# A hybrid S5 and retention layer on one core: a single-column product ahead of each S5 chunk's transposes, and four smaller moves

## The chip, the cores and the metric

The kernel runs on one core of a Trainium2 chip. The metric is the device time of one execution in microseconds (us); three executions of the kernel before gave 1423.64 to 1424.38, with a median of 1424.18. One more execution was profiled and took 1424.95, of which the profile's span is 1423.2.

## The reference, cut to what matters

One layer of a hybrid network works on 256 prompt tokens and on 8 samples of 8 tokens each, 320 in all, with D = 2048:

```python
h = rms_norm(x, norm_mix)
u, q, k, v, g = split(h @ w_in)            # 1024 columns each
bu = einsum(u in 64 groups of 16, b_bar)   # S5: a 64-dim complex state per group
xs = associative_scan(lam_bar, bu); y = Re(einsum(xs, c)) + d * u
y = gelu(y); s5_out = y * sigmoid(y @ w_glu + b_glu)
# retention: 8 heads, rotary positions, decay, group norm
scores = (rotary(q) @ rotary(k)) * mask
o = scores @ v + (q @ r) * q_decay;  r_new = r * decay + (k * k_decay) @ v
ret_out = silu(g) * group_norm(o)
x = x + concat(s5_out, ret_out) @ w_out
x = x + (silu(gate) * up) @ w_ffn_out      # gate, up = split(rms_norm(x) @ w_ffn_in)
```

All of it is float32; the S5 and retention states after the last token are outputs too.

## The kernel before, in words

Every large product is `weights x activations` with the 320 tokens as columns. A weight load brings 8 tiles of 128x128 (512 KB) into `raw`. ScalarE rounds it into `hi` (the CAST at L133), VectorE subtracts to get `lo` (L135), and TensorE runs three products per tile: hi with the rounded activations (L145), hi with their rest (L146), lo with the rounded ones (L147). `raw`, `hi` and `lo` have three buffers each, so a load waits until the subtraction three loads earlier has freed its `raw`, and that one waits until TensorE has freed its `lo`.

The input projection `w_in` is 40 blocks of 128 columns: 8 for u, then q, k, v, g for each of the 8 heads. Each block is 16 tiles, 48 products into `ps_p`. Between these products TensorE runs the small work: retention for 8 heads (`head_k`: transposes `pst`, scores `pss`; `head_v`: transposes `pst2`, outputs `po` and `psr`, transposes `pn`) and S5 for 8 chunks of 8 groups (`s5_chunk`). After it come w_out, the GLU, the FFN and the final norm, which the change doesn't touch.

An S5 chunk c goes like this. ScalarE copies its part of u to `up_`; SP writes that to DRAM (`via`, L586) and reads it back in eight transfers (L590) into `kst`, each into 16 of its 128 rows, which lays the four time steps of a window below one another. `kst` has two buffers. VectorE builds `bl` and `cl` from the chunk's parameters. After a delay `b1`, TensorE transposes `bl` into `pt` (four at L109), and ScalarE copies them to `bst`. After a further delay `b2` come the outputs of the chunk before (`s5_outputs`, products of `kst`, `toe` and `cl`, `xp` into `py`) and the chunk's own products of `bst` with `kst` into `pb`. The last columns of `pb` give the first block of `toe`; six transfers (L654) shift it into place. VectorE then scans (`s5_scan`). For the last chunk the outputs follow in the same function after a delay `scan`.

What sets the order: TensorE and POOL run in the order in which the program emits them. A planner emits it: `clk.now` adds an estimated cost for each product (0.4 per tile of a projection, 0.04 to 0.43 for the small ones), and generators such as `s5_chunk` and `head_k` come back at a due time (`yield DL[...]`: b1 14.2, b2 6.6, scan 17.8), when `run_due` finds them between two tiles. VectorE, ScalarE and SP are ordered by the framework with priorities (`tc.high_priority(offset=...)`, weight loads highest) and by `tc.issue_after`. SP issues all loads and transfers of the projection from one queue, in one order, and each instruction in it that must wait holds those behind it.

`make_identity` and `ones` are the constants for the transposes and for eight products (`warm_ps`, L118) that TensorE runs first of all. `rot` turns q and k of a head (three VectorE operations); `vsp` collects the sample part of v of two heads (L770).

Of the kernel before, what the change touches and what calls it, by code (L numbers as in the profile page):

```python
# [46 lines left out]
def hybrid_kernel(ctx, tc, xT, w_in, w_in4, w_out, w_glu, w_fi, w_fo, w_fot, gfr, vecs, s5p, bc, x0,  # L47
# [11 lines left out]


    ident = cst.tile([P, P], F32, name="ident")
    make_identity(nc, ident)
    ones = cst.tile([P, P], F32, name="ones")
    pool.memset(ones, 1.0)
    mhalf = cst.tile([P, 4], F32, name="mhalf")
    pool.memset(mhalf, -0.5)
    vec = cst.tile([P, vecs.shape[1]], F32, name="vec")
# [35 lines left out]
    def mm(cost, *a, **k):  # L103
        pe.matmul(*a, **k)
        clk.now += cost
# [471 lines left out]
    def s5_chunk(c):  # L577
# [42 lines left out]
            tbl = s5_table(c)  # L620
        bst = s5.tile([P, 4, P], F32, name="bst", tag="bst", bufs=1)
        pt = misc("pt")
        for i in range(4):
            tr(pt[:, P * i:P * i + P], bl[:, i // 2, i % 2].rearrange("p u e h -> p (u e h)"))
        with tc.high_priority(offset=EVAC):
# [3 lines left out]
        if c:  # L629
            while clk.now - used["misc"] < MISC:  # L630
                yield 0.4
            pending.pop()()
        pb = ps_b.tile([P, 2, 512], F32, name="pb", tag="pb", bufs=1)
        for i in range(4):
            for u in range(2):

# [20 lines left out]
        if c < 7:  # L657
            pending.append(lambda: s5_outputs(c, kst, cl, xp))
            return
        yield DL["scan"]  # L660
        while clk.now - used["misc"] < MISC:
            yield 0.4
        s5_outputs(c, kst, cl, xp)
# [61 lines left out]
    def rot_(ps, name):  # L725
        sw = mp.tile([P, N], F32, name="sw", tag="sw", bufs=1)
        act.copy(sw[0:64], ps[64:128])
        rot_t["keys"] = act.copy(sw[64:128], ps[0:64])
        a = mp.tile([P, N], F32, name=name, tag=name, bufs=1)
        tt(a, ps, csr[:, 0], MUL)  # L730
        tt(sw, sw, csr[:, 1], MUL)
        tt(a, a, sw, ADD)
        return a

    def head_k(h, q_, qg, k_, R):
# [25 lines left out]
    def head_v(h, v_, qg, rt, R):  # L761
        yield DL["v"] + (3.0 if h == 0 else 0.0)
        pst2 = misc("pst2")
        for i, s in enumerate(STARTS):
            tr(pst2[:, P * i:P * i + P], v_[:, s:s + P])
        vT = mp.tile([P, 3, P], F32, name="vT", tag="vT", bufs=1)
        with tc.high_priority(offset=EVAC):
            for i in range(3):
                act.mul(vT[:, i], pst2[:, P * i:P * i + P], rtok[:, i:i + 1])
        act.copy(vsp[64 * (h % 2):64 * (h % 2) + 64], vT[64:128, 2])  # L770
        last = act.copy(vs[:, h], vT[64:128, 2])
        if h == 0:
            rot_t["values"] = last
            with tc.issue_after(last.ins):
                s5_powers()
            start_chunk(0)
        yield DL["o"]
        kd, sm = R["kd"], R["sm"]

        po = ps_v.tile([P, 4, P], F32, name="po", tag="po", bufs=1)  # L780
        mm(0.22, po[:, 0], sm[:, 0:P], vT[:, 0], start=True, stop=True)
        mm(0.22, po[:, 1], sm[:, P:256], vT[:, 0], start=True, stop=False)
        mm(0.22, po[:, 1], sm[:, 256:384], vT[:, 1], start=False, stop=True)
        nt = 2 + h % 2
        if h % 2:
            two = (HS[h - 1], R)
            mm(0.22, po[:, 2], smp, vsp, start=True, stop=False, skip_group_check=True)
            for j in range(4):
                for g in range(2):
                    for u in range(2):  # L790
                        r = 64 * g + 32 * u
                        mm(0.06, po[r:r + 32, 2], two[g]["qg"][:, u, 32 * j:32 * j + 32],
                           two[g]["rt"][:, 4 * u + j], start=False, stop=j == 3, tile_position=(0, r),
                           skip_group_check=True)
        st = mp.tile([P, 3, 6], F32, name="st", tag="st", bufs=1)
        mv = mp.tile([P, 2, 3], F32, name="mv", tag="mv", bufs=1)[:, :, 0:nt]
        y = mp.tile([P, 2, 3], F32, name="gy", tag="gy", bufs=1)[:, :, 0:nt]
        with tc.high_priority(offset=GN):
            for i in range(nt):
                dve.bn_stats(st[:, i], po[:, i])  # L800
                dve.bn_aggr(mv[:, :, i], st[:, i])

        m_, t_, y_, w_ = mv[:, 0], mv[:, 1], y[:, 0], y[:, 1]
        pool.tensor_scalar(m_, m_, -1.0, None, MUL)
        pool.tensor_scalar(t_, t_, EPS, None, ADD)
        pool.tensor_tensor(y_, t_, mhalf[:, 0:nt], ALU.pow)
        pool.tensor_tensor(w_, y_, y_, MUL)
        pool.tensor_tensor(w_, w_, t_, MUL)
        pool.tensor_scalar(w_, w_, -0.5, 1.5, MUL, ADD)
        pool.tensor_tensor(y_, y_, w_, MUL)  # L810
        pool.tensor_tensor(w_, m_, y_, MUL)
        if h == 0:
            rot_t["first"]()
        on = mp.tile([P, 3, P], F32, name="on", tag="on", bufs=1)

        def normed():
            with tc.high_priority(offset=EVAC):
                for i in range(nt):
                    act.activation(on[:, i], po[:, i], AF.Identity, scale=y[:, 0, i:i + 1],
                                   bias=y[:, 1, i:i + 1])  # L820

        if h:
            normed()
        psr = misc("psr")
        mm(0.22, psr[:, :P], kd[:, 0], vT[:, 0], start=True, stop=False)
        mm(0.22, psr[:, :P], kd[:, 1], vT[:, 1], start=False, stop=True)
        rp = mp.tile([P, P], F32, name="rp", tag="rp", bufs=1)
        with tc.high_priority(offset=EVAC):
            act.copy(rp, psr[:, :P])
        sp.dma_start(rp_o[h], rp)  # L830
        t0 = clk.now
        if not h:

            for _ in range(2):
                cast = last_hi[0]
                while last_hi[0] is cast:
                    yield 0.4
            with tc.issue_after(last_hi[0].ins):
                normed()
        yield max(2.0, DL["c"] - (clk.now - t0))  # L840
        pn = misc("pn")
        for i in range(nt):
            tr(pn[:, P * i:P * i + P], on[:, i])

        R["fused"] = R.get("sgt") is not None
        parts = [(h, pn[:, 0:NP], slice(0, NP))]
        if h % 2:
            parts += [(h - 1 + g, pn[:, NP + 64 * g:NP + 64 * g + 64], slice(NP, N)) for g in range(2)]
        with tc.high_priority(offset=EVAC):
            for i, a_, sl in parts:  # L850
                if HS[i]["fused"]:
                    stt(retp[:, i, sl], a_, v("gn", i), HS[i]["sgt"][:, sl], MUL, MUL)
                else:
                    act.mul(retp[:, i, sl], a_, v("gn", i))
        if h % 2:
            for R_ in two:
                R_["gn"] = True
                if R_["fused"]:
                    R_["sg"] = True
# [16 lines left out]
    def do_q(h, ps=None):  # L876
        ps = proj(8 + 4 * h) if ps is None else ps
        R = HS[h]
        rt = mp.tile([P, NB, P], F32, name="rt", tag="rt", bufs=2)
        R["rt"] = rt  # L880
        for i in range(2 if h == 1 else min(h, 1)):
            i = i if h == 1 else h
            with tc.issue_after(last_raw[0].ins) if h == 1 else nullcontext():
                sp.dma_start(HS[i]["rt"], r0[i])
        mk = mp.tile([P, NP + P], F32, name="mk", tag="mk", bufs=2)
        n = NP + P if h % 2 else NP
        with nullcontext() if h else tc.issue_after(last_raw[0].ins):
            sp.dma_start(mk[:, 0:n], masks[h, :, 0:n])
        R["mk"] = mk
        q_ = rot(ps, "q_")  # L890
        pool.tensor_copy(qsp[:, 64 * (h % 2):64 * (h % 2) + 64], q_[:, NP:N])
        qg = qgs[h % 2]
        for u in range(2):
            tt(qg[:, u].rearrange("p (b w) -> p b w", w=40)[:, :, 0:NS],
               q_[:, NP + 32 * u:NP + 32 * u + 32].rearrange("p (b t) -> p b t", t=NS),
               gqt[:, h].unsqueeze(1).to_broadcast([P, 4, NS]), MUL)
        R.update(q_=q_, qg=qg)
        run_due()

    def do_k(h, ps=None):  # L900
        ps = proj(9 + 4 * h) if ps is None else ps
        R = HS[h]
        k_ = rot(ps, "k_")
        pool.tensor_tensor(kvf[:, h], k_[:, NP:N].rearrange("p (b t) -> p b t", t=NS),
                           kdt[:, h].unsqueeze(1).to_broadcast([P, NB, NS]), MUL)
        pool.tensor_copy(ksp[:, 64 * (h % 2):64 * (h % 2) + 64], k_[:, NP:N])
# [82 lines left out]
    def finish_norm():  # L989
# [4 lines left out]
        with tc.high_priority(offset=EVAC):  # L994
            act.copy(rbc, rps)
            tt(csr[:, 0], csr[:, 0], rbc, MUL)
            turned = dve.tensor_tensor(csr[:, 1], csr[:, 1], rbc, MUL)
            tt(u32[:, 0], ps0, rbc, MUL)
            tt(u32[:, 1], ps1, rbc, MUL)
        rot_t["ready"] = True  # L1000

        with tc.issue_after(turned.ins):
            s5_params2(exps[1])

    spawn(finish_norm(), DL["nm"])

# [538 lines left out]
```

## Time and profile before

| | |
|---|---|
| median of three runs | 1424.18 us (1423.64 to 1424.38) |
| the profiled execution | 1424.95 us |
| its span | 1423.2 us |
| TensorE busy | 1415.5 us, 99% of the span, 10376 records |
| VectorE busy | 957.9 us, 67% |
| ScalarE busy | 606.5 us, 43% |
| POOL busy | 122.8 us, 9% |
| DMA, 16 engines | 267.07 MB, mean 188 GB/s |

A row of a timeline gives the start, the duration, the engine, the line, the operation, output and inputs, shapes, the number of instructions in the row, and in brackets the idle time before it with what ended it. A row of the waits view names the engine and line that waited, what it waited for, the total, the number of times and the longest. A row of the windows view has the stretch and its length, busy time (and instructions) of TensorE, its weight loads, VectorE, ScalarE and POOL, then the granted TensorE clock, the DMA share and the rate. `SPq` rows are the issues of transfers on SP's queue, not the transfers themselves; `PEld` rows are TensorE's weight loads.

### The profile page before, as it was taken

Reading aid. Unit: us, or ns where it says so; the run is one execution under the profiler, and the core shown is the slowest. Engines: PE = TensorE matmul, PEld = TensorE weight load, DVE = VectorE, ACT = ScalarE, POOL = GpSimd, SP = SyncE. Lnnn points to the kernel's source line nnn. Section 1 sums busy time; section 2 is a strip of 40 time slices with the busy share of each in tenths; the row PEclk is TensorE's granted clock in tenths of the full one; section 3 lists DMA queues with packets and bytes.
Section 4 is the critical chain, followed back from the end, with each engine's and each line's share of the span. In section 5 each row is a group of like instructions: output and inputs, shape, how many; then the busy total and the mean of one; then the engine's idle time right before and its main releaser. Section 6 shows DMA issues by size and latency. Waiting matters only on the chain.

```text
span 1423.2 us, 26196 instructions
## 1 busy us (share of the span) xinstructions
PE 1415.5 (99%) x10376; PEld 1406.6 (99%) x10376; DVE 957.9 (67%) x1842; ACT 606.5 (43%) x973; POOL 122.8 (9%) x194
## 2 busy tenths in 40 slices
PE   9999999999999999999999999999999999999998
PEld 8999999999999999999999999999999999999998
DVE  7979878787557747777777545767644677655453
ACT  6654555555455443333333333333333333334553
POOL 7720111110000000100001000000000000000002
PEclk9999999999999999999999999999999999999999
DMA  8554555555644466675666446666545765445542
GB/s 278 170 187 158 163 174 157 171 163 157 218 156 151 164 209 228 221 253 201 245 206 231 136 148 238 233 216 235 170 146 175 255 233 190 159 157 184 154 143 75
DMA packets 102316, 267.07 MB, mean 188 GB/s; under 512 B 27377, under 2 KB 42033, under 8 KB 102193
## 3 DMA queue, kind: packets, MB, share of 16 engines
q1 hardware_dynamic: 101904, 265.01, 55.9%
q8 instruction: 81, 1.33, 0.4%
q10 hardware_dynamic: 288, 0.39, 0.1%
q14 instruction: 43, 0.34, 0.1%
HBM read 254.44 MB, written 10.52 MB: 186 GB/s over the span
## 4 chain that ended last, share of the span: by engine, by line
PE 96%; DVE 2%; DMA 1%; ACT 1%; issue 1%; POOL 0%; SPq 0%; POOLq 0%; DVEq 0%; ACTq 0%
PE ps_fg L147 7%; PE ps_fu L147 7%; PE ps_fu L146 7%; PE ps_fg L146 7%; PE ps_fg L145 7%; PE ps_fu L145 7%; PE ps_fo L147 7%; PE ps_fo L145 7%; PE ps_fo L146 7%; PE ps_p L145 6%; PE ps_p L147 6%; PE ps_p L146 6%; PE ps_o L145 2%; PE ps_o L146 2%; PE ps_o L147 2%; PE ps_t L1342 1%
## 5 line engine op out<-in xcount | busy, mean ns | idle before, releaser
L133 ACT CAST hi<-raw 128x1024 fp32r<-128x1024 f32 (+1 forms) x410 | 397.8, 971 | 684.2 <-PE ps_fg L146 182.3
L135 DVE TENSOR_TENSOR lo<-raw,hi 128x1024 fp32r<-128x1024 f32 (+1 forms) x410 | 462.8, 1129 | 304.2 <-ACT hi L133 301.3
L147 PE MATMUL ps_fg<-hhi,lo 128*128 128x320 f32 x704 | 218.0, 310 | 0.0
L147 PE MATMUL ps_fu<-hhi,lo 128*128 128x320 f32 x704 | 217.9, 310 | 0.0
L145 PE MATMUL ps_fg<-hhi,hi 128*128 128x320 f32 x704 | 217.9, 310 | 0.0
L146 PE MATMUL ps_fu<-hlo,hi 128*128 128x320 f32 x704 | 217.9, 310 | 0.0
L145 PE MATMUL ps_fu<-hhi,hi 128*128 128x320 f32 x704 | 217.9, 310 | 0.0
L146 PE MATMUL ps_fg<-hlo,hi 128*128 128x320 f32 x704 | 217.9, 310 | 0.0
L145 PE MATMUL ps_fo<-ahl,hi 128*128 128x320 f32 x671 | 208.0, 310 | 0.0
L147 PE MATMUL ps_fo<-ahl,lo 128*128 128x320 f32 x671 | 207.7, 310 | 0.0
L146 PE MATMUL ps_fo<-ahl,hi 128*128 128x320 f32 x671 | 207.7, 310 | 0.0
L145 PE MATMUL ps_p<-xhi,hi 128*128 128x320 f32 x560 | 177.3, 317 | 0.0
L147 PE MATMUL ps_p<-xhi,lo 128*128 128x320 f32 x560 | 173.3, 309 | 0.0
L146 PE MATMUL ps_p<-xlo,hi 128*128 128x320 f32 x560 | 173.1, 309 | 0.0
L147 PEld LDWEIGHTS ps_fg<-hhi,lo 128*128 128x128 f32 x704 | 132.2, 188 | 0.0
L146 PEld LDWEIGHTS ps_fu<-hlo,hi 128*128 128x128 f32 x704 | 132.2, 188 | 0.0
L146 PEld LDWEIGHTS ps_fg<-hlo,hi 128*128 128x128 f32 x704 | 132.2, 188 | 0.0
L145 PEld LDWEIGHTS ps_fg<-hhi,hi 128*128 128x128 f32 x704 | 132.2, 188 | 0.0
L147 PEld LDWEIGHTS ps_fu<-hhi,lo 128*128 128x128 f32 x704 | 132.1, 188 | 0.0
L145 PEld LDWEIGHTS ps_fu<-hhi,hi 128*128 128x128 f32 x704 | 132.1, 188 | 0.0
L146 PEld LDWEIGHTS ps_fo<-ahl,hi 128*128 128x128 f32 x671 | 126.0, 188 | 0.0
L147 PEld LDWEIGHTS ps_fo<-ahl,lo 128*128 128x128 f32 x671 | 126.0, 188 | 0.0
(476 smaller groups left out, 2117.8 us busy)
## 6 DMA issues: line engine op xcount, KB each, us to landing
raw<-w_fi SPq DMA_DIRECT2D x176, 512.0 KB, 4.2
raw<-w_in SPq DMA_DIRECT2D x79, 512.0 KB, 4.1
raw<-w_fo SPq DMA_DIRECT2D x61, 512.0 KB, 3.5
raw<-w_out SPq DMA_DIRECT2D x32, 512.0 KB, 3.7
hi<-vd SPq DMA_DIRECT2D x32, 512.0 KB, 5.4
lo<-vd SPq DMA_DIRECT2D x32, 512.0 KB, 5.2
raw<-w_fo SPq DMA_DIRECT2D x61, 192.0 KB, 2.4
rt<-r SPq DMA_DIRECT2D x8, 512.0 KB, 5.2
```

Of the source, the lines that this page charges most:

```text
L133: cast = act.copy(hi[:, :m], raw[:, :m])
L135: last_lo[0] = dve.tensor_tensor(lo[:, :m], raw[:, :m], f(hi[:, :m]), SUB)
L145: pe.matmul(ps, hi, xhi[:, k], start=k == 0, stop=False)
L146: pe.matmul(ps, hi, xlo[:, k], start=False, stop=False)
L147: pe.matmul(ps, lo, xhi[:, k], start=False, stop=k == nk - 1)
L1342: pe.matmul(ps[0:m, 0:TC], a3[:, x_, k, s:s + m], w_[:, k], start=k == 0 and x_ == 0 and w_ is whi, stop=k == FCT - 1 and w_ is wlo)
```

## The change

Five pieces. `ones` is set on VectorE, ahead of `make_identity`, instead of on POOL. In chunks 1 to 7, a product of a single column (3x1, from `toe` and the first column of this chunk's `kst`) is put ahead of the transposes `pt`; its output column in `pb` is written over later, and `pb` is allocated there for it. It reads all that the eight L590 transfers of this chunk and the six `toe` transfers of the chunk before write. The planner counts 0.06 for it. The last chunk's delay ahead of its outputs grows by 1.2. A part of the S5 parameters (`s5_params2`) and the scaled queries of the first head are issued behind the first head's keys. And the copy to `vsp` gets a higher priority in odd heads.

```diff
+    ones = cst.tile([P, P], F32, name="ones")
+    dve.memset(ones, 1.0)
     make_identity(nc, ident)
-    ones = cst.tile([P, P], F32, name="ones")
-    pool.memset(ones, 1.0)
...
         pt = misc("pt")
+        pb = ps_b.tile([P, 2, 512], F32, name="pb", tag="pb", bufs=1)
+        if c:
+            mm(0.06, pb[0:CH - 1, 1, 4 * NC:4 * NC + 1], toe[:, 0, 0:CH - 1, 0], kst[:, 0, 0:1], start=True, stop=True)
         for i in range(4):
             tr(pt[:, P * i:P * i + P], bl[:, i // 2, i % 2].rearrange("p u e h -> p (u e h)"))
...
             pending.pop()()
-        pb = ps_b.tile([P, 2, 512], F32, name="pb", tag="pb", bufs=1)
...
-        yield DL["scan"]
+        yield DL["scan"] + 1.2
...
-        tt(a, a, sw, ADD)
+        rot_t["turned"] = dve.tensor_tensor(a, a, sw, ADD)
...
-        act.copy(vsp[64 * (h % 2):64 * (h % 2) + 64], vT[64:128, 2])
+        with tc.high_priority(offset=EVAC if h % 2 else 0):
+            act.copy(vsp[64 * (h % 2):64 * (h % 2) + 64], vT[64:128, 2])
...
-                dve.bn_aggr(mv[:, :, i], st[:, i])
+                aggr = dve.bn_aggr(mv[:, :, i], st[:, i])
...
         if h == 0:
             rot_t["first"]()
+            with tc.issue_after(aggr.ins):
+                R["scaled_q"]()
...
-        for u in range(2):
-            tt(qg[:, u].rearrange("p (b w) -> p b w", w=40)[:, :, 0:NS],
...
-        R.update(q_=q_, qg=qg)
+        def scaled_q():
+            for u in range(2):
+                tt(qg[:, u].rearrange("p (b w) -> p b w", w=40)[:, :, 0:NS],
...
+        R.update(q_=q_, qg=qg, scaled_q=scaled_q)
+        if h:
+            scaled_q()
...
         k_ = rot(ps, "k_")
+        if not h:
+            with tc.issue_after(rot_t["turned"].ins):
+                s5_params2(exps[1])
...
-            turned = dve.tensor_tensor(csr[:, 1], csr[:, 1], rbc, MUL)
+            tt(csr[:, 1], csr[:, 1], rbc, MUL)
...
-        with tc.issue_after(turned.ins):
-            s5_params2(exps[1])
```

On TensorE, at chunk 2, the order before was this (`ps_p` is the projection, `pt` the transposes of the chunk):

```order
L145 MATMUL ps_p<-xhi,hi 128x320
L146 MATMUL ps_p<-xlo,hi 128x320
L147 MATMUL ps_p<-xhi,lo 128x320
L109 MATMUL pt<-ident,bl 128x128 x4
L145 MATMUL ps_p<-xhi,hi 128x320
```

and now it is this, with the semaphores that an instruction waits for behind it (DMAHW0 to 7 count the transfers):

```order
L145 MATMUL ps_p<-xhi,hi 128x320
L146 MATMUL ps_p<-xlo,hi 128x320
L147 MATMUL ps_p<-xhi,lo 128x320
L104 MATMUL pb<-kst,toe 3x1 [waits DMAHW4_49,DMAHW3_49,DMAHW5_49,DMAHW2_49,DMAHW6_49,DMAHW1_49,DMAHW7_49,DMAHW0_49,PE_49]
L109 MATMUL pt<-ident,bl 128x128 x4
L145 MATMUL ps_p<-xhi,hi 128x320
```

The new product stands between the projection and the transposes and waits for transfers; the `py` and `pb` products of this chunk follow later, as before. In chunks 6 and 7 the transposes also stand three products (one tile) earlier than they did.

On SP's queue the eight L590 transfers of chunk 2 stand like this, before and now alike (`raw<-w_in` is a weight load, which waits for VectorE):

```order
L132 DMA raw<-w_in 128x1024 [waits DMAHW5_49,DVE_49]
L654 DMA toe<-toe 48x4x16 [waits DMAHW6_49]
L590 DMA kst<-via 16x4x80 [waits DMAHW7_49]
L590 DMA kst<-via 16x4x80 [waits DMAHW0_49]
L590 DMA kst<-via 16x4x80 [waits DMAHW1_49]
L132 DMA raw<-w_in 128x1024 [waits DMAHW2_49,DVE_49]
L590 DMA kst<-via 16x4x80 [waits DMAHW3_49]
L590 DMA kst<-via 16x4x80 [waits DMAHW4_49]
L132 DMA raw<-w_in 128x1024 [waits DMAHW5_49,DVE_49]
L590 DMA kst<-via 16x4x80 [waits DMAHW6_49]
```

Only the line of the `toe` transfer differs (L656 now). The last of the transfers stands behind a weight load. In chunk 5 one of them stands behind the last weight load where two did, in chunk 6 one where three did; behind these, `via` and `mk` of the next steps stand ahead of a weight load in some chunks where they stood behind it.

On VectorE, the first head's queries and keys before (`scrt` and `lp` belong to the S5 parameters):

```order
L180 TENSOR_TENSOR q__727<-pb_157,csr 128x320
L180 TENSOR_TENSOR sw<-sw,csr 128x320
L180 TENSOR_TENSOR lp<-rr,ecs 128x32 x2
L180 TENSOR_TENSOR q__727<-q__727,sw 128x320
L180 TENSOR_TENSOR scrt<-prm 128x32 x2
L180 TENSOR_TENSOR qg_111<-q__727,gqt 128x4x8 x2
L180 TENSOR_TENSOR scrt<-scrt 128x32
L135 TENSOR_TENSOR lo<-raw,hi 128x1024
L180 TENSOR_TENSOR k__737<-ps_p,csr 128x320
L180 TENSOR_TENSOR sw<-sw,csr 128x320
L428 RECIPROCAL scrt<-scrt 128x32
L180 TENSOR_TENSOR k__737<-k__737,sw 128x320
```

and now:

```order
L180 TENSOR_TENSOR q__721<-pb_157,csr 128x320
L180 TENSOR_TENSOR sw<-sw,csr 128x320
L734 TENSOR_TENSOR q__721<-q__721,sw 128x320
L135 TENSOR_TENSOR lo<-raw,hi 128x1024
L180 TENSOR_TENSOR k__729<-ps_p,csr 128x320
L180 TENSOR_TENSOR sw<-sw,csr 128x320
L734 TENSOR_TENSOR k__729<-k__729,sw 128x320
```

The keys follow the queries with one subtraction between; the S5 operations and `qg` stand behind them.

More of the change, by code (lines that the diff above doesn't have):

```diff
@@ L892, in do_q @@
         qg = qgs[h % 2]
-        for u in range(2):
-            tt(qg[:, u].rearrange("p (b w) -> p b w", w=40)[:, :, 0:NS],
-               q_[:, NP + 32 * u:NP + 32 * u + 32].rearrange("p (b t) -> p b t", t=NS),
-               gqt[:, h].unsqueeze(1).to_broadcast([P, 4, NS]), MUL)
-        R.update(q_=q_, qg=qg)
+        def scaled_q():
+            for u in range(2):
+                tt(qg[:, u].rearrange("p (b w) -> p b w", w=40)[:, :, 0:NS],
+                   q_[:, NP + 32 * u:NP + 32 * u + 32].rearrange("p (b t) -> p b t", t=NS),
+                   gqt[:, h].unsqueeze(1).to_broadcast([P, 4, NS]), MUL)
+        R.update(q_=q_, qg=qg, scaled_q=scaled_q)
+        if h:
+            scaled_q()
         run_due()
```

## The prediction

> **What bounds the kernel now.** I read the page's first part, then its chain, then the waits of TensorE alone.
>
> ```profile
> span 1423.2 us, 26196 instructions
> PE 1415.5 (99%) x10376; PEld 1406.6 (99%) x10376; DVE 957.9 (67%) x1842; ACT 606.5 (43%) x973; POOL 122.8 (9%) x194
> PE 96%; DVE 2%; DMA 1%; ACT 1%; issue 1%; POOL 0%; SPq 0%; POOLq 0%; DVEq 0%; ACTq 0%
> ```
>
> TensorE is busy 1415.5 of 1423.2 us and carries 96% of the chain that ends last. So whatever lets TensorE stand still lengthens the kernel by the same amount, and whatever only hurries another engine is worth no more than the TensorE waits that it removes. Those are few:
>
> ```profile
> PE py L977 <- ACT hi L967: 0.9, 2, 0.6
> PE pst L109 <- DVE k__737 L180: 0.3, 1, 0.3
> PE pst L109 <- ACT kd L743: 0.3, 1, 0.3
> PEld po L104 <- ACT vsp L770: 0.2, 1, 0.2
> ```
>
> None of them is on a DMA. The S5 transfers cost nothing today because their first reader stands late enough. Chunk 2, on TensorE and then on SP's queue, shows by how little:
>
> ```profile
> 144.68 0.60 PE L109 MATMUL pt<-ident,bl 128*128 128x128 f32 x4
> 152.47 0.51 PE L104 MATMUL py<-kst,toe 64*64 64x80 f32 x16
> 153.35 0.88 PE L104 MATMUL pb<-kst,bst 64*64 64x80 f32 x32
> 148.65 0.35 SPq L132 DMA_DIRECT2D raw<-w_in  x1
> 149.04 0.43 SPq L590 DMA_DIRECT2D kst<-via  x1
> DMA to landing us min/median/max: 1.6/3.4/4.5
> ```
>
> The four transposes pt start at 144.68. The last transfer of this chunk's kst is issued at 149.04, behind a weight load, and at the median landing time it is in at 149.04 + 3.4 = 152.44. The first product that reads it (in pb) comes at 153.35. It is in time by 0.9 us, and 7.8 us too late for anything that would stand ahead of pt.
>
> **The single-column product.** The new 3x1 product reads kst of its own chunk in all 128 rows (so all eight transfers) and stands directly ahead of pt in chunks 1 to 7. TensorE runs its instructions in order, so behind the waiting product stand pt, the rest of the projection (the ps_p products) and, through the lo and hi buffers that these release, the next weight loads. What it moves is the wait for kst: from the py and pb products, 7.8 us behind pt, to ahead of pt. For each chunk I take the issue of the last kst transfer, add the median landing of 3.4, and subtract the start of pt. The rows, TensorE first, chunks 1 and 3 to 7:
>
> ```profile
> 111.44 0.60 PE L109 MATMUL pt<-ident,bl 128*128 128x128 f32 x4
> 180.67 0.60 PE L109 MATMUL pt<-ident,bl 128*128 128x128 f32 x4
> 216.01 0.60 PE L109 MATMUL pt<-ident,bl 128*128 128x128 f32 x4
> 251.09 0.60 PE L109 MATMUL pt<-ident,bl 128*128 128x128 f32 x4
> 286.55 0.60 PE L109 MATMUL pt<-ident,bl 128*128 128x128 f32 x4
> 322.07 0.60 PE L109 MATMUL pt<-ident,bl 128*128 128x128 f32 x4
> 94.09 1.06 SPq L590 DMA_DIRECT2D kst<-via  x2
> 178.66 0.90 SPq L590 DMA_DIRECT2D kst<-via  x2
> 217.82 0.43 SPq L590 DMA_DIRECT2D kst<-via  x1
> 252.17 1.34 SPq L590 DMA_DIRECT2D kst<-via  x2
> 287.49 1.37 SPq L590 DMA_DIRECT2D kst<-via  x3
> 317.32 1.84 SPq L590 DMA_DIRECT2D kst<-via  x4
> ```
>
> Chunk 1: issued by 95.15, landed by 98.6, pt at 111.44: no pause. Chunk 2: 7.76. Chunk 3: the second of two is issued at about 179.13, so 179.13 + 3.4 - 180.67 = 1.86. Chunk 4: 217.82 + 3.4 - 216.01 = 5.21. In chunks 5 and 6 the change leaves one kst transfer behind the last weight load, where two and three stood, so the first issue of the group counts: 252.17 + 3.4 - 251.09 = 4.48, and, since pt of chunks 6 and 7 also moves 0.44 (three products) forward, 287.49 + 3.4 - 286.11 = 4.78. Chunk 7: the last of four is issued at about 318.73, so 318.73 + 3.4 - 321.63 = 0.5. The sum is 24.6 us.
>
> Does the kst transfer itself come sooner or later once TensorE pauses? The weight load ahead of it waits for DVE's subtraction that frees its raw buffer, and that subtraction needs the lo buffer that an earlier TensorE product releases. By the order of the changed program that product stands 12 products ahead of the new one in chunks 2 and 4 and 20 ahead in chunks 5 and 6. So the pause can't feed on itself, but it can't vanish either. The shortest way round goes by these rows of the page:
>
> ```profile
> L133 ACT CAST hi<-raw 128x1024 fp32r<-128x1024 f32 (+1 forms) x410 | 397.8, 971 | 684.2 <-PE ps_fg L146 182.3
> L135 DVE TENSOR_TENSOR lo<-raw,hi 128x1024 fp32r<-128x1024 f32 (+1 forms) x410 | 462.8, 1129 | 304.2 <-ACT hi L133 301.3
> SPq L132 <- DVE lo L135: 826.0, 332, 10.9
> ```
>
> A cast of 0.97, a subtraction of 1.13, then 0.39 from the load's issue to that of kst (149.04 - 148.65) and 3.4 to land: 5.9 us. Less 12 products of 0.147 (53.14 - 52.99 in the projection) that is 4.1 in chunks 2 and 4, less 20 of them 3.0 in chunks 5 and 6; with 0.75 for chunks 3 and 7 the bottom is 15.0. The top takes the longest landing, 4.5, in six chunks: 24.6 + 6.6 = 31.2. I take 24.6, because the load of chunk 2 goes out 3.97 us after pt although its releasing product ran 1.8 us before pt: DVE is late with its own S5 work there, and a pause of TensorE doesn't shorten that work.
>
> Each pause also ends with a restart. The one stall of this kind in the trace is the first head's keys:
>
> ```profile
> 52.98 0.67 DVE L180 TENSOR_TENSOR k__737<-k__737,sw 128x320 f32<-128x320 f32 x1
> 52.99 0.31 PE L146 MATMUL ps_p<-xlo,hi 128*128 128x320 f32 x1
> 53.14 0.31 PE L147 MATMUL ps_p<-xhi,lo 128*128 128x320 f32 x1
> 53.79 0.41 PE L109 MATMUL pst<-ident,k__737 128*128 128x128 f32 x2 [0.35 <-DVE k__737 L180]
> ```
>
> k is done at 53.65 and TensorE starts at 53.79: 0.14 us. Over six pauses that is 0.8.
>
> **The clock after a pause.** Two places show TensorE after idling, its first eight products and the end of the kernel:
>
> ```profile
> 1.12 3.47 PE L118 MATMUL warm_ps<-ones 128*128 128x512 f32 x8 [1.12 <-POOL ones L64]
> 1415.66 2.47 PE L118 MATMUL warm_ps<-ones 128*128 128x512 f32 x10
> 1418.80:1420.60 1.80, 0.00 (x1) 0.00 (x0) 0.63 (x2) 0.21 (x1) 0.72 (x1) 1.00 0.58 172
> 1420.70:1423.00 2.30, 0.00 (x0) 0.00 (x0) 0.00 (x0) 0.00 (x0) 0.00 (x0) 0.50 0.47 155
> ```
>
> From 1418.80 no product runs, and 1.9 us later the granted clock is 0.50. The same 128x512 product takes 3.47 / 8 = 0.43 us at the start and 2.47 / 10 = 0.25 at the end, so coming back costs about 3.47 x (1 - 0.25 / 0.43) = 1.5 us. I charge it to the four pauses over 3 us: 6.0. Its bounds are 0 (the clock doesn't fall in a pause) and five times 1.5 = 7.5 (the 1.86 us of chunk 3 counts too).
>
> [...]
>
> **What the change saves.** The products themselves: the nearest row is a single-column one with a full set of weights.
>
> ```profile
> 36.12 0.72 PE L104 MATMUL ps_r<-ones,u 128*128 128x1 f32 x6
> 36.70 0.39 PE L145 MATMUL ps_pv<-xhi,hi 128*128 128x320 f32 x1
> ```
>
> Six entries (three products, each in two passes) in 0.58 us is 0.19 a product; with 3 weight columns it can be less, down to 0.03. I take 0.16: seven cost 1.1. Against that, the py products no longer carry the waits on the S5 transfers' queues:
>
> ```profile
> PEld py L104 <- issue: 1.5, 8, 0.2
> L104 PEld LDWEIGHTS po<-rt,qg x128: 105/110/111, 94.2 to 316.8; 128*32 128x32 f32 x128
> ```
>
> Eight py blocks lose 1.5 us in which TensorE's weight loads wait for nothing but their own queue, 0.19 each. Seven of them stand behind a new product, so at most 1.3 goes; I take 0.9, since TensorE's products still run beside a part of it (between 0 and 1.3). Keys of the first head: the change puts k's three rotary operations right behind a single subtraction on DVE, and the S5 parameter operations and the scaled queries behind them. The wait ahead of pst was 53.79 - 53.14 - 0.147 = 0.50 and goes. What was late next, kd (0.3), follows k and goes as well. The vsp copy ahead of its neighbour on ACT removes the 0.2 above. Sum 0.9 + 0.5 + 0.3 + 0.2 = 1.9, less 1.1 for the products: a gain of 0.8 (between -1.1 and 2.1).
>
> At nothing I cost three edits. The memset of ones on DVE instead of POOL frees the eight first products up to 1.1 us sooner, but the work behind them waits for the first weights and x (the py waits above), so these cover it; were they gone it would be worth 1.1. The scan delay of 1.2 for the last outputs leaves py of chunk 7 at its place on TensorE, since the seven costs of 0.06 had moved the clock of the planner. The scaled queries of the first head, deferred to about 60, are first read on TensorE at 94.2; the deferred S5 parameters feed bl, for which TensorE waits nowhere in its list of waits; the projection covers both.
>
> **Sum.** 24.6 + 0.8 + 6.0 - 0.8 = 30.6 on the profiled 1424.95, so 1455.5. The median of the runs, 1424.18, is 0.8 lower: 1455.
>
> **The rivals.**
> *The clock stays full.* Pauses as computed, no cold restarts: 1424.2 + 24.6 + 0.8 - 0.8 = 1449. For it: no pause of this length inside the kernel has been seen. Against: the drop 1.9 us after the last product.
> *The loads catch up.* If in the pause DVE gets ahead of TensorE, the next chunk's loads go out near the shortest way round: 15.0 + 0.8 - 0.8 + three restarts of 1.5 gives 1424.2 + 19.5 = 1443.7. For it: SP's loads wait 826 us for DVE's subtractions in all, so they follow TensorE closely. Against: only three buffers, so one pause gives a lead of one block, which is used up again before the next chunk 35 us later.
> *The transfers are in time (the other side).* If the weight load ahead of the last kst transfers isn't late in the changed kernel, the product finds kst landed and only the 0.8 is left: 1423.4. It decides once the last issue comes 3.4 us ahead of pt, in chunk 2 by 7.8 us. For it: in some chunks via and mk are now issued ahead of a weight load, and that reshuffles the queue; chunks 1 and 7 are nearly there. Against: in chunk 2 the queue is the same to the last kst transfer, and the releasing product, 12 products or 1.8 us before pt, leaves the shortest way round of 5.9 us no room.
>
> **How the numbers follow.** My forecast has 0.67, the full clock 0.14, the catching-up loads 0.11, the transfers in time 0.08. The range takes the bounds of the unknown costs: below 15.0 of pauses, no restart of the clock and no gain over the products, 1424.2 + 15.8 = 1440, less 1 for the gain's top; above 31.2 + 0.8 + 7.5 - 0.8 = 38.7, so 1463, to which 1 is added for the gain's bottom. 1439 to 1464 leaves out the last rival and little more. Within 0.2% (2.8 us), about what a measurement of this kernel can tell from no change, only the last rival lies, mostly: 0.07; faster 0.02; slower 0.91.
>
> **What would show it.** In the changed trace, pb products with wait rows on kst or a DMA at 144 to 153, 216 to 221 and their like, of 7.8, 5.2, 4.5 and 4.8 us (each later by the pauses before); granted clock under 1 in the stretch behind each; py blocks about 0.15 shorter; no wait for k ahead of pst at 53. I am wrong if TensorE has no wait over 1 us between 100 and 330, or if the last kst issue of chunk 2 comes before 141.

## The result, and the profile after

The changed kernel takes 1461.81 us (median, 1460.48 to 1462.55) against 1424.07 before (five executions of each): ratio 1.0264, 95% interval 1.0249 to 1.0279. It is 37.7 us slower. Its profiled execution took 1462.55, of which the span is 1460.8. The top of its page and the chain that ended last:

```profile
span 1460.8 us, 26197 instructions
PE 1427.0 (98%) x10390; PEld 1416.8 (97%) x10390; DVE 959.5 (66%) x1843; ACT 608.1 (42%) x973; POOL 133.3 (9%) x193
PE 86%; DVE 7%; DMA 2%; issue 2%; ACT 1%; SPq 1%; POOL 1%; POOLq 0%; DVEq 0%
```

TensorE's busy time grew by 11.5 us although only seven small products were added. The span grew by 37.6, so the other 26 us are time in which it stood still. Both are in the rows below. First the waits of TensorE, which had none on a DMA before:

```profile
PE pb L104 <- DMA via<-up__2355: 8.1, 1, 8.1
PE pb L104 <- DMA kst<-via: 7.8, 3, 4.8
PE pb L104 <- DMA mk<-masks: 5.8, 1, 5.8
PE pb L104 <- DMA via<-up__4365: 5.5, 1, 5.5
```

They are six waits, 27.2 us, all at the new product. Some rows name `via` or `mk`: these are transfers that the product doesn't read. The view names what landed closest ahead of the end of the wait, and in chunk 2 these were issued within 2 us behind the last kst transfer. Chunk 2 in TensorE's timeline:

```profile
143.34 0.31 PE L147 MATMUL ps_p<-xhi,lo 128*128 128x320 f32 x1
151.77 0.19 PE L104 MATMUL pb<-kst,toe 128*3 128x1 f32 x2 [8.13 <-DMA via<-up__2355]
```

the same time on SP's queue:

```profile
147.44 0.35 SPq L132 DMA_DIRECT2D raw<-w_in  x1
147.83 0.43 SPq L590 DMA_DIRECT2D kst<-via  x1
```

and the landing of all kst transfers:

```profile
DMA to landing us min/median/max: 1.8/3.4/4.7
```

The weight load goes out 3.8 us after TensorE fell idle (151.77 - 8.13 = 143.64), much as it went out 4.0 us after pt had started before; the kst transfer follows it, and the product starts 3.9 us behind that issue. VectorE's lateness was not shortened by the pause: in both traces the subtraction that frees the buffer ends 0.03 us ahead of the load.

The windows view shows the second part, the granted clock (the column ahead of the last two) behind the pauses of chunks 2, 3 and 4, and then over the whole stretch:

```profile
151.70:153.70 2.00, 1.93 (x10) 1.92 (x11) 0.00 (x0) 0.59 (x1) 0.00 (x0) 0.50 0.13 40
191.80:192.70 0.90, 0.90 (x9) 0.87 (x9) 0.00 (x0) 0.36 (x2) 0.39 (x2) 1.00 1.01 341
193.00:196.00 3.00, 3.00 (x13) 3.00 (x13) 0.66 (x1) 2.02 (x4) 0.00 (x0) 0.50 0.83 322
196.40:198.40 2.00, 2.00 (x15) 2.00 (x15) 0.17 (x1) 0.00 (x0) 0.00 (x0) 1.00 0.41 128
234.60:236.20 1.60, 1.55 (x10) 1.54 (x10) 0.00 (x0) 0.28 (x1) 0.00 (x0) 0.50 0.02 8
110.00:380.00 270.00, 242.58 (x2286) 236.75 (x2286) 185.47 (x381) 128.46 (x291) 38.42 (x66) 0.94 0.44 136
```

Behind five of the six pauses the products run at half the clock for 3.4 to 6 us, chunk 3 included. To cost it I subtracted the start of the same product in this trace and in one without these pauses (the kernel with a column of ones, below), once right behind the restart and once at the end of the slow stretch; what that difference grew by is the price of the slow stretch.

| chunk | pause predicted | wait measured | slow stretch costs |
|---|---|---|---|
| 2 | 7.76 | 8.1 | 1.6 |
| 3 | 1.86 | 2.5 | 1.6 |
| 4 | 5.21 | 5.8 | 2.7 |
| 5 | 4.48 | 4.8 | 1.9 |
| 6 | 4.78 | 5.5 | 2.6 |
| 7 | 0.5 | 0.5 | 0 |
| sum | 24.6 | 27.2 | 10.4 |

Together 37.6 us. The gains and the products themselves nearly cancel, as the experiments below show.

### The profile page after: what moved, and what is told of

It is laid out like the page before. It is cut to its first block, busy times and chain, and to the rows that moved or that the text cites. A ratio compares the mean times of both kernels' runs of the same rounds, so it can differ in the third digit from the quotient of the medians.

```text
span 1460.8 us, 26197 instructions
## 1 busy us (share of the span) xinstructions
PE 1427.0 (98%) x10390; PEld 1416.8 (97%) x10390; DVE 959.5 (66%) x1843; ACT 608.1 (42%) x973; POOL 133.3 (9%) x193
## 4 chain that ended last, share of the span: by engine, by line
PE 86%; DVE 7%; DMA 2%; issue 2%; ACT 1%; SPq 1%; POOL 1%; POOLq 0%; DVEq 0%
PE ps_fu L146 7%; PE ps_fg L147 7%; PE ps_fu L147 7%; PE ps_fg L146 7%; PE ps_fg L145 7%; PE ps_fu L145 7%; PE ps_fo L145 7%; PE ps_fo L147 7%; PE ps_fo L146 7%; PE ps_p L145 3%; PE ps_p L146 3%; PE ps_p L147 3%; DVE lo L135 3%; PE ps_o L145 2%; PE ps_o L146 2%; PE ps_o L147 2%
## 5 line engine op out<-in xcount | busy, mean ns | idle before, releaser
L145 PE MATMUL ps_p<-xhi,hi 128*128 128x320 f32 x560 | 180.9, 323 | 0.0
L146 PE MATMUL ps_p<-xlo,hi 128*128 128x320 f32 x560 | 176.4, 315 | 0.0
L147 PE MATMUL ps_p<-xhi,lo 128*128 128x320 f32 x560 | 176.4, 315 | 0.0
L146 PEld LDWEIGHTS ps_fo<-ahl,hi 128*128 128x128 f32 x671 | 126.0, 188 | 0.0
L145 PEld LDWEIGHTS ps_fo<-ahl,hi 128*128 128x128 f32 x671 | 125.9, 188 | 0.0
```

The costliest lines, as they stand in the source:

```text
L145: pe.matmul(ps, hi, xhi[:, k], start=k == 0, stop=False)
L146: pe.matmul(ps, hi, xlo[:, k], start=False, stop=False)
L147: pe.matmul(ps, lo, xhi[:, k], start=False, stop=k == nk - 1)
```

## The experiments

Every kernel ran beside the kernel before on the same chip.

**Without the product.**

```diff
-            mm(0.06, pb[0:CH - 1, 1, ...], toe[:, 0, 0:CH - 1, 0], kst[:, 0, 0:1], start=True, stop=True)
+            clk.now += 0.06
```

> The changed kernel without the seven single-column products; the planner's 0.06 for each is kept, so TensorE's order is otherwise the changed one. Theory (the products' wait for kst makes all of the loss, pauses and cold clock): before 1424.1, less the 1.47 us by which the changed kernel is ahead at the first head's values, less 0.2 for vsp: 1422.4, and no TensorE wait over 1 us between 100 and 380. Rival (the moved operations or another order of SP's queue bear a part of the loss): over 1426.

Measured 1423.82 (1423.09 to 1424.28), ratio 0.9997, interval 0.9989 to 1.0006. All of the loss went with the product. The expected 1.7 of gain is not there in the times, only 0.3 that the interval doesn't tell from nothing. TensorE's waits of this kernel are these, with no k or kd among them any more (among those of its weight loads vsp is gone, and one on kd of 0.3 is left where there was one of 0.4):

```profile
PE warm_ps L118 <- DVE ones L63: 1.0, 1, 1.0
PE py L990 <- ACT hi L980: 0.8, 1, 0.8
PE py L990 <- DVE xhi L180: 0.5, 1, 0.5
```

**The product alone, in the kernel before.** Only the hunk with `pb` and the product is applied; the other four edits are left out.

> The kernel before with nothing but the single-column product (its order on TensorE and on SP's queue is that of the changed kernel; the memset, the first head's order on VectorE, vsp and the last outputs stay as before). Theory (the product makes all of the loss, the other edits make 0.3 to 0.9 of gain): 1461.8 + 0.3 to 0.9 = 1462.1 to 1462.7. Rival (the product only pauses because the other edits moved work on VectorE): under 1455.

Measured 1461.66 (1460.78 to 1461.89), ratio 1.0262 (1.0247 to 1.0278): within the noise of the whole change, and 0.4 under the expected bounds. The product is the loss, and the other edits move nothing in it that the times show.

**What the product waits for: a column of ones in place of kst.**

```diff
-  toe[:, 0, 0:CH - 1, 0], kst[:, 0, 0:1]
+  toe[:, 0, 0:CH - 1, 0], ones[:, 0:1]
```

> The single-column products stay where they are, but multiply toe with a column of ones in place of a column of kst, so they wait for the toe transfers of the chunk before and no longer for kst. Theory (the kst wait is the loss): 1422.4 plus seven products of 0.22, 1423.9. Rival (the wait for toe, or the products themselves, hold TensorE): 1440 or more.

Measured 1425.80 (1425.04 to 1426.20), ratio 1.0010 (1.0001 to 1.0019). The pauses are gone, so the wait for toe isn't the cause. It is 1.9 over the expected 1423.9, and 2.0 above the kernel without the product where 1.5 was expected. In the trace each product delays the start of pt by 0.22 us, but the projection product behind pt by 0.27; seven of these make 1.9.

**Fewer rows, fewer transfers.** The product over rows 0 to 63, then over rows 0 to 95.

```diff
-  toe[:, 0, 0:CH - 1, 0], kst[:, 0, 0:1]
+  toe[0:64, 0, 0:CH - 1, 0], kst[0:64, 0, 0:1]     # or 0:96
```

> The changed kernel with the product over the first 64 rows alone, so it waits for the first four kst transfers of its chunk, which land 2 to 5 us before it (0.5 after it in chunk 5). Theory (only transfers that land after the product's place cost): 1425.8 as with a column of ones, plus 0.5, less some of the 0.86 that py blocks wait: 1425.5 to 1426.3. Rival (reading kst of the own chunk costs the pause, whichever rows): 1450 to 1462.

Measured 1427.21 (1426.23 to 1427.86), ratio 1.0021 (1.0012 to 1.0031): 0.9 above the expected bounds, since two waits on kst of 1.8 in all were left where I had worked out 0.5.

> The changed kernel with the product over the first 96 rows, so it waits for six of the eight transfers. The sixth lands after the product's place by about 2.2 us in chunk 2, 1.5 in 4, 0.7 in 5, 1.5 in 6 and 0.5 in 7. Theory (the pause is that landing, and the clock falls only behind longer pauses): 1425.8 + 6.4 less 0.5 for py blocks = 1431.7, granted clock 1.00 but for chunk 2 at most. Rival (the clock falls behind each such pause, 1.5 to 2 us each): 1437 to 1441.

Measured 1433.51 (1433.21 to 1434.98), ratio 1.0065 (1.0048 to 1.0082). The wait of TensorE at the product sums to the 6.4 us worked out, though by luck: the four pauses are 1.6, 1.8, 0.9 and 2.1 in chunks 2, 4, 5 and 6 where 2.2, 1.5, 0.7 and 1.5 were expected, and the 0.5 of chunk 7 isn't there:

```profile
PE pb L104 <- DMA kst<-via: 6.4, 4, 2.1
```

In the windows view of the same kernel, around the products of chunks 2, 4, 5 and 6:

```profile
140.00:150.00 10.00, 8.38 (x61) 8.10 (x59) 4.53 (x6) 5.26 (x9) 1.96 (x5) 1.00 0.31 100
217.00:224.00 7.00, 5.16 (x28) 5.09 (x28) 2.12 (x4) 3.19 (x8) 0.00 (x0) 0.76 0.59 184
254.00:262.00 8.00, 7.11 (x79) 6.53 (x78) 4.69 (x11) 4.77 (x11) 0.00 (x0) 1.00 0.49 155
293.00:300.00 7.00, 6.00 (x35) 6.00 (x36) 2.44 (x5) 3.12 (x7) 0.00 (x0) 0.76 0.38 111
```

The time is 1.8 above the theory and at least 3.5 under the rival: in this execution the clock fell behind two of the four pauses (0.76 in those windows), at about 1.6 each, and these are chunks 4 and 6, not chunk 2 as the theory allowed. The profiled execution is the slowest of the four, 1434.98 at a mean clock of 0.997; the other three took 1433.2 to 1433.5 at 0.998 and 0.999. With four, six and eight transfers the time goes 1427.2, 1433.5, 1461.8, and the wait 1.8, 6.4, 27.2. The loss grows with how late the last transfer read lands, not with the product.

**The product later.** The same product, with kst and toe, directly ahead of the py products.

```diff
+            pe.matmul(pb[0:CH - 1, 1, ...], toe[:, 0, 0:CH - 1, 0], kst[:, 0, 0:1], start=True, stop=True)
             pending.pop()()
```

> The same products, with kst, but put directly ahead of the py products, some 7.5 us later, where kst has landed. Theory (the place decides, not the product): 1422.4 plus 7 x 0.2 less up to 0.9 for py products without waits: 1422.9 to 1423.9, no wait over 1 us at them. Rival (a product that gathers all the waits costs a pause wherever it stands): 1430 or more.

Measured 1424.47 (1423.89 to 1425.02), ratio 1.0003 (0.9994 to 1.0011). Against the kernel before that is no difference that the times can tell, but it is 0.65 over the kernel without the product and 0.6 over the expected bounds. In the trace of this kernel the stretch from the projection product ahead of product, py and pb to the one behind them takes 2.50 us in six of the seven chunks, where with py and pb alone it took 2.37 in chunk 1 and mostly 2.52 in the others before. Chunk 2 takes 3.09, with one wait of 0.5 at the product: there the product starts 4.0 us behind the last kst issue, so even this place comes a little ahead of the last landing.

**The transfers earlier.** The kst transfers of chunks 1 to 7 above the weight loads in priority.

```diff
+                with tc.high_priority(offset=3200 if c else 0):
                     sp.dma_start(kst[64 * i + 16 * e:64 * i + 16 * e + 16], ...)
```

> The changed kernel, with the kst transfers of chunks 1 to 7 at a higher priority than the weight loads: all eight of a chunk stand in a row on SP's queue, 4 to 7 weight loads ahead of where the last one stood, some 20 us before the product. Theory (the pause is the landing of the last kst transfer behind a late weight load): no pause, full clock, 1423.8 + 1.5 for seven products less 0.86 for py blocks without waits: 1424.5, plus up to 1 per chunk where eight transfers hold a weight load. Rival (any gathered wait on eight queues pauses TensorE): over 1450.

Measured 1455.86 (1455.60 to 1456.37), ratio 1.0223 (1.0208 to 1.0238). By the numbers this is the rival's result. TensorE's longest waits in this kernel are these:

```profile
PE pb L104 <- DMA raw_bc<-bc: 9.3, 2, 5.4
PE pb L104 <- DMA toe<-toe: 8.2, 3, 4.6
PE pb L104 <- DMA via<-up__3348: 5.4, 1, 5.4
```

at its product in chunk 2:

```profile
149.50 0.19 PE L104 MATMUL pb<-kst,toe 128*3 128x1 f32 x2 [5.43 <-DMA raw_bc<-bc]
```

and at SP's queue ahead of it:

```profile
119.25 4.27 SPq L591 DMA_DIRECT2D kst<-via  x8
145.22 0.35 SPq L132 DMA_DIRECT2D raw<-w_in  x1
145.61 1.24 SPq L657 DMA_DIRECT2D toe<-toe  x2
```

All eight kst transfers now leave at 119, but in the new order the last two toe transfers of the chunk before slid behind a weight load, to 145.61, and the product waits for them too: it starts at 149.50, 3.2 us behind the second one's issue. My expectation had left out that the product reads fourteen transfers, not eight. This run alone doesn't decide between the theory and the rival. The next does.

**Both kinds of transfer earlier.** As the run before, and the six toe transfers raised for every chunk as they were for the last.

```diff
-        with tc.high_priority(offset=4 * EVAC if c == 7 else 0):
+        with tc.high_priority(offset=4 * EVAC):
```

> As the kernel with the kst transfers first, and the six toe transfers of each chunk raised too (they had slid behind weight loads there, and the product waits for them as well: TensorE still stood 5.5, 2.7, 5.4, 4.0, 4.8 and 1.0 us, then on toe). Theory (the pause is the landing of whichever of the fourteen transfers goes out last): no wait over 0.5 us at the product, clock full, 1423.8 + 1.5 - 0.9 = 1424.5, plus 0 to 2 us per chunk if fourteen transfers in a row hold the weight loads for 6.6 us, then shown as waits of ps_p products on hi or lo. Rival (a product that gathers many queues' waits pauses TensorE by itself): 1450 or more with waits at the product.

Measured 1432.82 (1431.99 to 1434.50), ratio 1.0063 (1.0049 to 1.0077). At the product there is no wait left; the longest waits behind the start-up are now elsewhere, and none of these is on a weight load's hi or lo for over 0.3 us:

```profile
PE py L104 <- ACT retp L860: 3.1, 1, 3.1
PE pss L104 <- POOL ksp L920: 1.2, 1, 1.2
PE ps_p L147 <- DVE lo L135: 0.3, 1, 0.3
```

So a product with the waits of fourteen transfers costs its 0.3 us and nothing more if they have landed, and the rival falls. The kernel is still 8.4 us over the unchanged one, 7.5 in the profiled execution (1431.99). Most of that is in the trace: a py of the last chunk waits 3.1 us for ScalarE's retp, a score product 1.2 for POOL, the row above has 0.3, and behind the 3.1 the clock stands at half for one stretch of 3.41 us (336.87 to 340.28), at most 1.7 of time. With 1.9 for the products, less 0.9 for pb, that is 7.3. So here, too, the clock fell, against the expectation. That the raised transfers push this other work back is likely and not shown; the loads that were named for it did not stall TensorE by more than 0.3.

**The clock.** Extra products without use, written over later, fill the pauses of chunks 2 to 6 of the changed kernel: 32, 9, 22, 18 and 20 of them, and in a second kernel 36, 12, 26, 21 and 25.

```diff
+            for _ in range((0, 0, 32, 9, 22, 18, 20, 0)[c]):
+                pe.matmul(pb[:, 1], onesr, onesr.unsqueeze(1).to_broadcast([P, 4, P]), start=True, stop=True)
```

> The changed kernel with extra products without use (128x512, written over later) directly ahead of the single-column ones in chunks 2 to 6: 32, 9, 22, 18 and 20 of them, each 0.23 us at the full clock, so they fill all but 0.4 to 0.9 us of each pause. Theory (10.2 us of the loss are products at half clock behind the pauses): 1461.8 - 10.2 = 1451.6, granted clock 1.00 from 110 to 380. Rival (the clock doesn't follow TensorE's idle time, or the slow stretch has another cause): 1460 to 1463; if the extra products lengthen the pauses: over 1463.

Measured 1455.16 (1452.86 to 1456.42), ratio 1.0221 (1.0205 to 1.0237). Its profiled execution (1452.86) has the clock full throughout in the windows view, against 0.94 above:

```profile
110.00:380.00 270.00, 264.95 (x2453) 254.61 (x2453) 194.00 (x400) 134.54 (x299) 29.00 (x66) 1.00 0.47 144
```

It has a rest of the waits, the longest group of which is this:

```profile
PE pb L104 <- DMA kst<-via: 1.5, 2, 1.1
```

TensorE does 101 products more and the kernel is 6.7 us faster in the medians, 9.7 in the profiled executions. The median is 3.6 over the expected 1451.6. The rest of the pauses of chunks 2 to 6 is 0.5 to 1.1 us long, a little more than planned. Of the other executions the record has the mean granted clock: the profiled one has 1.000, those of 1454.79 and 1455.52 have 0.999, the slowest (1456.42) has 0.998. One stretch of 3.41 us at half clock would take 3.41 x 0.5 / 1455 = 0.0012 off the mean, so by this estimate a fall of the clock in the slower ones fits. The second kernel leaves less idle time:

> As the kernel with the pauses filled by extra products, with 36, 12, 26, 21 and 25 of them (120 x 0.23 = 27.6 us in place of 23.2), which leaves at most 0.3 us idle at each. Theory (the medians of that kernel lay 2.3 above its profiled execution because in most executions the clock fell once or twice in the rest of the pauses): 1423.8 + 0.6 + 27.6 + 1 = 1453.0, executions within 1 us of each other. Rival (the spread has nothing to do with idle time; the extra products only add length): 1455.2 + 2 = 1457 or more, with a spread as wide as before (3.5 us).

Measured 1453.94 (1453.56 to 1455.12), ratio 1.0213 (1.0197 to 1.0228), a spread of 1.6 instead of 3.6. More products again made it no slower (1.2 faster in medians of four executions each, whose ranges overlap), where the rival had it 2 slower. That speaks for the theory, but not for all of it: 0.9 is left over the 1453.0, the spread is more than the 1 us expected, and the slowest execution, 1455.12, has a clock of 1.000, so what it is longer by has another cause, which stays open. The slow stretches are worth some 8 to 10 us of the 37.7.

**The memset.** The kernel without the product, and with the memset of ones on POOL as before.

> The changed kernel without the single-column products and with the memset of ones back on POOL; only the order of the first head's keys, vsp and the last outputs is changed. Theory (the three TensorE waits that go are 0.5 + 0.2 + 0.2 = 0.9, and the memset's move costs about 0.6 at the start): 1423.2. Rival (the memset is worth nothing, and 0.9 isn't reached for another reason): 1423.8, as with the memset on VectorE.

Measured 1424.03 (1423.09 to 1424.27), ratio 0.9997 (0.9988 to 1.0006). This is the rival's case: where the memset stands changes nothing that can be measured.

## Why the prediction was right, and where its sizes were off

The forecast was 1455 and slower; measured were 1461.8. By its steps:

*The wait moves ahead of pt.* Right. The product alone makes the loss (product alone 1461.66, all but the product 1423.82), and it does so by the last transfer of kst that stands behind a late weight load: the wait scales with the transfers read, and vanishes when all fourteen are landed, or but for 0.5 us when the product stands 7 us later.

*24.6 us of pauses, and 0.8 of restarts.* Mechanism right, 27.2 measured. The term that was mis-sized is the landing: I added the median over all kst transfers, 3.4, but in chunks 2, 4, 5 and 6 the last one stands directly behind a 512 KB weight load. There the product starts 3.9 to 4.2 us after the issue (3.94 after 147.83 in chunk 2), where 3.4 + 0.14 was taken; in chunk 3, with another kst transfer between the load and the last one, it is 3.9, in chunk 7 3.3. Of the kst transfers whose landing the changed kernel's trace holds, the eight directly behind a load take 3.9 in the median, the other 25 take 3.2. Over the six pauses the measured waits, which hold the restarts too, lie 0.3 on average over 24.6 / 6 + 0.14. The place of the issues was closer: in chunk 2 it came 4.2 us behind the product's turn, where 149.04 - 144.68 = 4.4 was taken; the largest miss is 0.5 (chunk 5), and all six together are 0.6 early.

*The clock, 6.0.* Right that the clock falls with these pauses, too small by 4.4: five pauses instead of four, chunk 3's 2.5 us among them, which stood as the upper bound only, and 1.6 to 2.7 each instead of 1.5. The 1.5 came from the kernel's start, where the eight slow products take 3.5 us; chunk 4's slow stretch lasts from 234.65 to 240.6, 6 us. The 10.4 is also over the term's upper bound of 7.5. That the time still came out inside the range is in part luck: the upper bound of the pauses, 31.2, had 4.0 to spare, which covered it. (The range's ends allow 1 us for the gain; with the gain's own bounds, 2.1 and -1.1, they would be 1438 and 1465.) "The clock stays full", the first rival, falls by the rows at 0.50; the kernels whose pauses were filled with products ran at 1.00.

*The gain.* In the trace the sizes are nearly as worked out. The first head's wait for k (0.5) is gone, and so are 0.2 each at kd, where 0.3 was taken, and vsp; the timeline of TensorE in the changed kernel:

```profile
52.40 0.31 PE L147 MATMUL ps_p<-xhi,lo 128*128 128x320 f32 x1
52.55 0.38 PE L109 MATMUL pst<-ident,k__729 128*128 128x128 f32 x2
53.65 0.55 PE L109 MATMUL pst<-ident,v__741 128*128 128x128 f32 x3
```

pst stands directly behind ps_p. Of the chain of the kernel before, a py stretch and the pb stretches of chunks 1, 2 and 4:

```profile
152.54 0.99 PE py L104 x48
120.51 1.14 PE pb L104 x48
153.53 1.29 PE pb L104 x48
224.76 1.34 PE pb L104 x48
```

and of the changed kernel's chain, chunks 2 and 3, with a row of the weight loads' waits:

```profile
162.37 1.14 PE pb L104 x48
202.52 1.14 PE pb L104 x48
161.38 0.99 PE py L104 x48
PEld py L104 <- issue: 1.8, 9, 0.3
```

In the chain of the changed kernel pb is 1.14 wherever it stands. Summed over the chunks, py and pb together are 0.86 shorter. That 0.9 was taken is luck: the prediction took it from the weight loads' waits at py, and py is 0.99 in both kernels, with those waits still there (1.8 in nine, where there were 1.5 in eight). What got shorter is pb, which reads this chunk's kst; with the column of ones, which doesn't wait for kst, the times show no such gain: 1425.80 is 2.0 over the kernel without the product, for products that cost 1.9. The product was taken at 0.16, below the 0.19 of the nearest row and above a lower end of 0.03, which was my estimate and which no run shows for it; it costs 0.27 in that kernel's trace, 1.9 for seven, so even without any pause the product costs more than it saves. The first head's 0.9 isn't visible in the times: without the product the median is 0.3 lower, with an interval from 1.6 lower to 0.9 higher. In the profiled executions it is there (1424.95 before, 1423.74 and 1424.06 with the edits and without the product); the profiled execution before lies 0.9 above its own median, so how much of it is the start of that one execution stays open.

*The other rivals.* That the loads catch up over the pauses and bring 1443.7 didn't happen: each last issue lies within 0.5 us of the place taken for it. That the transfers are in time fell with the first row of the waits.

## What to carry to other kernels

A product that gathers waits is worth only what the waits cost where they stood (here 0.12 us per chunk, 0.86 over seven, for a price of 0.27), and it must stand behind the landing of everything that it reads; on an engine that is 99% busy, the time by which the last transfer lands behind its place is lost whole. Ask for the issue of the last transfer in the queue, not the first, and take the landing time of that one: directly behind a 512 KB load it was 3.9 here, against 3.4 in the median of all. And if pauses like the five of 2.5 to 8.1 us here can't be avoided on TensorE, count the slow stretches behind them too; these added 10.4 us, 38%, to the pauses.

## What the runs showed of the hardware that was not expected

In these runs the clock didn't go by the length of the pause alone. A pause of 1.84 us (chunk 4 of the kernel with six transfers) was followed by a slow stretch, one of 1.96 (chunk 3 of the product alone) was not:

```profile
218.91 0.19 PE L104 MATMUL pb<-kst,toe 96*3 96x1 f32 x2 [1.84 <-DMA kst<-via]
192.55 0.19 PE L104 MATMUL pb<-kst,toe 128*3 128x1 f32 x2 [1.96 <-DMA kst<-via]
```

And in chunk 3 of the changed kernel the clock was still full from 191.80 to 192.70, when TensorE was at work again, and fell to 0.50 after that: here the pause is paid for once it is over.

The windows view, cut finely enough, gives the times at which the clock changes. In the changed kernel they are 148.53, 155.36, 192.90, 196.32, 233.86, 240.69, 274.82, 281.65, 319.20 and 326.02; from each to the next it is 3.41 us or a whole number of times that. The slow stretch of chunk 3 is one such step long, those of chunks 2, 4, 5 and 6 are two. Cut into steps of this length, counted from a change of the clock, the traces show a difference between the two cases above. The first pause lies within one step, and the next step runs at half clock:

```profile
215.79:219.20 3.41, 1.57 (x13) 1.30 (x12) 2.84 (x7) 0.93 (x2) 0.00 (x0) 1.00 0.42 148
219.21:222.62 3.41, 3.41 (x16) 3.41 (x16) 0.00 (x0) 1.96 (x6) 0.00 (x0) 0.50 0.89 270
```

The second is split between two steps, and the clock stays full through the one after them:

```profile
188.47:191.88 3.41, 2.13 (x34) 1.67 (x24) 1.39 (x7) 0.70 (x2) 1.25 (x3) 1.00 0.65 202
191.88:195.29 3.41, 2.74 (x21) 2.73 (x22) 0.00 (x0) 1.90 (x5) 1.07 (x6) 1.00 0.81 256
195.29:198.70 3.41, 3.41 (x25) 3.41 (x24) 1.71 (x2) 1.32 (x2) 0.00 (x0) 1.00 0.59 206
```

Three more steps, the first two of the changed kernel, the third of the kernel with both kinds of transfer earlier:

```profile
227.04:230.45 3.41, 1.78 (x13) 1.51 (x11) 3.35 (x8) 1.43 (x2) 0.00 (x0) 1.00 0.49 157
233.87:237.28 3.41, 2.63 (x13) 2.62 (x14) 0.00 (x0) 1.31 (x4) 0.00 (x0) 0.50 0.09 32
336.87:340.28 3.41, 2.77 (x76) 2.69 (x76) 2.73 (x5) 2.84 (x8) 0.00 (x0) 0.50 0.44 154
```

Behind the step with TensorE busy for 1.57 of 3.41 us the clock was at half; behind the one with 1.78 it stayed full for a step more. At half clock, the step with 2.63 was followed by another one at half, and the one with 2.77 by full clock. In these cases the outcome goes with the busy time of the step ahead, where it doesn't go with the length of the pause. What it would be between these numbers, or in another kernel, no run shows.
